# The final RMSNorm of a hybrid decoder: sums spread by one product, the root by Ln and Exp, VectorE's factors in PSUM, and the steps of a finished chunk written earlier

## The chip, the cores and the metric

The kernel runs on one core of a Trainium2 chip. The metric is the device time of one execution, in microseconds; smaller is better. The core's engines work side by side, each on its own list of instructions in order: TensorE (PE in the profile) multiplies matrices from SBUF into PSUM, VectorE (DVE), ScalarE (ACT) and GpSimd (POOL) work element by element, and SyncE (SP) issues the transfers between the chip's memory and SBUF. They wait for each other through semaphores.

## What is computed

One inference step of a small decoder: a Mamba-2 layer with a squared-ReLU MLP, then a layer of sliding-window attention with another MLP, for 1024 new prompt positions and 64 sample positions, each 1024 features wide. All that matters here is the very end, the norm of the stream after the second MLP:

```python
def rmsnorm(x, w):
    xf = x.astype(jnp.float32)
    xf = xf * lax.rsqrt(jnp.mean(xf * xf, axis=-1, keepdims=True) + EPS)
    return (xf * w.astype(jnp.float32)).astype(x.dtype)
...
    y_prompt = rmsnorm(hp, final_norm_w)
    y_sample = rmsnorm(hs, final_norm_w)
```

So each position needs the mean of the squares of its 1024 features, the inverse root of it, and a scaling of the 1024 features by that factor and by the weights.

## The kernel before

**Layout.** Features lie on the 128 partitions, positions along the free dimension: the stream `hh` is 128 x 8 x 1088, eight feature tiles (numbered u = 0 to 7) of 1088 positions. The positions are cut into three chunks, c = 0, 1 and 2, of 384, 384 and 320. A sum over features is therefore a sum over the eight tiles (VectorE) and over the partitions (a product with a matrix of ones on TensorE).

**The stage around the change.** The last block of the second MLP's down projection (`down_block`, `down`, `down_unit`, line 949) makes, for each chunk and tile, a group of twelve products into one PSUM tile `g`; the operands are split in two parts, so each of four weights enters through three products (lines 205 to 207). VectorE then adds the PSUM tile to `hh` (line 949); that is called eviction below. Tiles 0 to 3 are made for all chunks in turn; then the tail makes tiles 4 to 7 of chunk 0, of chunk 1, of chunk 2. The PSUM tiles `g` come from a ring of seven banks (`gps`, with three banks and four more), handed out in the order in which the code is written; a bank is free again when its last reader is through.

**What hangs on each eviction.** `final(c, u)` is called after each. After every odd tile up to 5 ScalarE squares a pair of tiles (`n3`), VectorE adds the squares into `acc`, and ScalarE multiplies the pair by its weights; tiles 6 and 7 are squared one by one into `sq` and get their weights later. For chunk 2, the square of tile 7 is not added but enters the sum over partitions as a second operand.

**The end of a chunk.** `final_rs` sums over the partitions: three products per chunk, each with 128 positions of `acc` as the stationary operand and a column of ones (line 1770), so that the sums lie as columns, 128 positions on the partitions. ScalarE takes the square root of the 128 x 3 values (line 1772), VectorE the reciprocal (1773), and three scalings of the identity give diagonal matrices `dg` (1776). `final_bc` multiplies ones with these (1787), which spreads each position's factor over all 128 rows of a PSUM tile, and ScalarE copies that into `rs` in SBUF (1789). `final_scale` multiplies a pair of tiles by the factor and sends it out (SyncE, line 1803): the pairs k = 4 and k = 0 are GpSimd's, k = 6 (with its weights, line 1799) and k = 2 are VectorE's (1802); for chunk 2, k = 0 is VectorE's as well. GpSimd always reads the factor from `rs`; VectorE reads it from `rs` for chunks 0 and 1, from PSUM for chunk 2.

**What sets the order.** The code is written in one sequence, and a scheduler with its own cost model places each engine's instructions, with the order of writing as the priority. Before, the end of chunk c - 1 is written at three places of chunk c: `final_rs` at tile 5, `final_bc` and all scalings at tile 7. The end of chunk 2 follows at its own tile 7.

Of the kernel before, what the change touches and what calls it, by code (L numbers as in the profile page):

```python
# [11 lines left out]
AF = mybir.ActivationFunctionType  # L12
ALU = mybir.AluOpType
# [4 lines left out]
P = 128  # L18
D = 1024
# [123 lines left out]
class Kernel:  # L143
# [1578 lines left out]
    def final(self, c, u, hts, chs):  # L1722

        nc = self.nc
        n = chs[c][1]
        h = hts[c]
        if c > 0 and u == 5:
            self.final_rs(c - 1, chs)
        if c > 0 and u == 7:
            self.final_bc(c - 1, chs)  # L1730
        if u % 2 and u < 6:
            sq = self.n3()[:, :, :n]
            nc.scalar.activation(out=sq, in_=h[:, u - 1:u + 1, :n], func=AF.Square)
            if u == 1:
                acc = self.fin("acc", 3, n)
                self.acc[c] = [acc]
                nc.vector.tensor_tensor(out=acc, in0=sq[:, 0], in1=sq[:, 1], op=ALU.add)
            else:
                acc = self.acc[c][0]
                for j in range(2):  # L1740
                    nc.vector.tensor_tensor(out=acc, in0=acc, in1=sq[:, j], op=ALU.add)

            for k in (u - 1, u):
                nc.scalar.mul(out=h[:, k, :n], in_=h[:, k, :n], mul=self.ncol(4)[:, k:k + 1])
        elif u >= 6:
            sq = self.fin("sq", 2, n)
            nc.scalar.activation(out=sq, in_=h[:, u, :n], func=AF.Square)
            if u == 6 or c < 2:
                nc.vector.tensor_tensor(out=self.acc[c][0], in0=self.acc[c][0], in1=sq, op=ALU.add)
            else:  # L1750
                self.acc[c].append(sq)
        if c > 0 and u == 7:
            for k, e in ((4, nc.gpsimd), (6, nc.vector), (0, nc.gpsimd), (2, nc.vector)):
                self.final_scale(c - 1, k, e, hts, chs)
        if c == 2 and u == 7:
            self.final_rs(c, chs)
            self.final_bc(c, chs)
            for k, e in ((6, nc.vector), (4, nc.gpsimd), (0, nc.vector), (2, nc.vector)):
                self.final_scale(c, k, e, hts, chs)

    def final_rs(self, c, chs):

        nc = self.nc
        n = chs[c][1]
        ms = self.gps()[:, :3]
        r = self.fin("rt", 2, 3)
        for b in range(3):
            o = min(b * P, n - P)
            for q, a in enumerate(self.acc[c]):
                nc.tensor.matmul(out=ms[:, b:b + 1], lhsT=a[:, o:o + P], rhs=self.ones_d[:, 0:1], start=(q == 0),  # L1770
                                 stop=(q == len(self.acc[c]) - 1))
        nc.scalar.activation(out=r, in_=ms, func=AF.Sqrt, bias=self.eps1)
        nc.vector.reciprocal(out=r, in_=r)
        dg = self.fin("dg", 2, 3 * P).rearrange("p (b t) -> p b t", b=3)
        for b in range(3):
            nc.vector.tensor_scalar(out=dg[:, b], in0=self.ident, scalar1=r[:, b:b + 1], scalar2=float(D),
                                    op0=ALU.mult, op1=ALU.mult)
        self.acc[c] = dg

    def final_bc(self, c, chs):  # L1780

        nc = self.nc
        n = chs[c][1]
        ps = self.gps()[:, :n]
        for b in range(3):
            o = min(b * P, n - P)
            nc.tensor.matmul(out=ps[:, o:o + P], lhsT=self.ones_d, rhs=self.acc[c][:, b], start=True, stop=True)
        rs = self.fin("rs", 2, n)
        nc.scalar.copy(out=rs, in_=ps)
        self.acc[c] = {nc.gpsimd: rs, nc.vector: ps if c == 2 else rs}  # L1790

    def final_scale(self, c, k, e, hts, chs):
        nc = self.nc
# [290 lines left out]
```

## Time and profile before

| | |
|---|---|
| median of the runs | 2852.68 us (3 runs, 2851.2 to 2852.72) |
| the profiled execution's own time | 2850.09 us |
| its span, first to last instruction | 2848.4 us |
| mean granted TensorE clock | 0.995 |
| output transfers of the final norm | 8 of 384 KB, 4 of 320 KB |
| last eviction starts | 2832.20 us |
| last scaling ends (VectorE) | 2843.79 us |

Times inside the span are counted from its start. A timeline row gives start, length, engine, line of the kernel, operation, tile written and tiles read, and in brackets the idle time of the engine before it and whom it waited for. A group of rows gives the count, the busy time with the mean in ns, and the idle time before. Products are pipelined: a row of TensorE is longer than the distance to the next, and a float32 product appears as two rows. KB in the table are of 1024 bytes.

### The profile page before, as it was taken

The numbers are of one execution on the slowest core, as the hardware profiler recorded it, in microseconds if no ns is written. First come the engines' busy times: TensorE is split into PE (matmuls) and PEld (weight loads), VectorE is DVE, ScalarE is ACT, GpSimd is POOL, SyncE is SP. The second block draws the span as 40 slices with busy tenths as digits, with TensorE's granted clock in tenths as the row PEclk, the third lists the DMA queues.
The fourth block names the chain that finished last, engine by engine and source line by source line (L and its number), as shares of the span: only waits on it lengthen the run. The fifth ranks groups of instructions, "written<-read, shape, count | busy, mean of one in ns | idle before, by whom it ended". The sixth has DMA issues, their size and how long they took to land.

```text
span 2848.4 us, 51380 instructions
## 1 busy us (share of the span) xinstructions
PE 2791.9 (98%) x19895; PEld 2692.3 (95%) x19895; DVE 2078.6 (73%) x3615; ACT 1389.7 (49%) x2719; POOL 471.0 (17%) x659
## 2 busy tenths in 40 slices
PE   8999999989999999999999999999999999999997
PEld 7999999979989999999999999988989999999997
DVE  6788888886768786666578875676688666567786
ACT  6555555545654255445343334555555444523333
POOL 3355555551000100000000022110110000000011
PEclk9999999999999999999999999999999999999999
DMA  4344444457655224533654523446553354533432
GB/s 140 94 127 123 119 124 124 124 145 249 246 206 181 91 93 133 176 133 131 246 197 174 192 99 104 165 171 240 182 194 110 132 183 146 226 111 127 145 113 71
DMA packets 219468, 433.42 MB, mean 152 GB/s; under 512 B 30728, under 2 KB 128392, under 8 KB 216648
## 3 DMA queue, kind: packets, MB, share of 16 engines
q1 hardware_dynamic: 219224, 430.14, 45.5%
q8 instruction: 157, 2.57, 0.4%
q14 instruction: 87, 0.71, 0.1%
HBM read 302.71 MB, written 128.32 MB: 151 GB/s over the span
## 4 chain that ended last, share of the span: by engine, by line
PE 86%; DVE 5%; DMA 5%; ACT 2%; issue 2%; POOL 0%; SPq 0%; DVEq 0%; ACTq 0%; POOLq 0%
PE g L206 12%; PE g L205 12%; PE g L207 12%; PE ma L205 4%; PE ma L207 4%; PE ma L206 4%; PE mc L207 4%; PE mc L206 4%; PE mc L205 4%; PE md L206 3%; PE md L207 3%; PE mb L207 3%; PE mb L206 3%; PE mb L205 3%; PE md L205 3%
## 5 line engine op out<-in xcount | busy, mean ns | idle before, releaser
L205 PE MATMUL g<-S,w 128*128 128x384 f32 (+2 forms) x1584 | 529.7, 335 | 4.7 <-DMA w<-ws_up 3.2
L206 PE MATMUL g<-S,w 128*128 128x384 f32 (+2 forms) x1584 | 531.5, 336 | 0.0
L207 PE MATMUL g<-S,w 128*128 128x384 f32 (+2 forms) x1584 | 527.4, 333 | 0.0
L205 PEld LDWEIGHTS g<-S,w 128*128 128x128 f32 x1584 | 298.5, 188 | 7.3 <-issue 4.7
L1078 ACT CAST w<-s 128x384 fp32r<-128x384 f32 (+1 forms) x272 | 150.6, 557 | 315.3 <-PE mc L207 57.9
L206 PEld LDWEIGHTS g<-S,w 128*128 128x128 f32 x1584 | 298.8, 189 | 3.0 <-issue 2.4
L207 PEld LDWEIGHTS g<-S,w 128*128 128x128 f32 x1584 | 299.4, 189 | 2.1 <-issue 1.7
L1329 POOL TENSOR_TENSOR hh<-hh,us 128x552 f32<-128x552 f32 (+1 forms) x24 | 42.5, 1790 | 1531.0 <-DVE us L1305 877.0
L205 PE MATMUL ma<-S,w 128*128 128x276 f32 (+1 forms) x808 | 234.1, 290 | 5.0 <-DVE us L1305 3.8
L206 PE MATMUL ma<-S,w 128*128 128x276 f32 (+1 forms) x808 | 233.8, 289 | 0.3 <-DVE S L1267 0.3
L207 PE MATMUL ma<-S,w 128*128 128x276 f32 (+1 forms) x808 | 234.0, 290 | 0.0
L1079 DVE TENSOR_TENSOR w<-s,w 128x384 fp32r<-128x384 f32 (+1 forms) x272 | 166.4, 615 | 80.8 <-ACT w L1078 80.7
L1078 ACT CAST w<-raw 128x384 fp32r<-128x384 f32 (+1 forms) x204 | 112.2, 557 | 183.9 <-PE mc L207 57.8
L171 ACT CAST w<-raw 128x1024 fp32r<-128x1024 f32 x96 | 100.7, 1049 | 142.3 <-PE g L206 52.8
L206 PE MATMUL g<-R,w 128*128 128x384 f32 (+2 forms) x480 | 158.3, 330 | 0.0
L205 PEld LDWEIGHTS ma<-S,w 128*128 128x128 f32 x808 | 152.5, 189 | 5.8 <-issue 4.1
L205 PE MATMUL g<-R,w 128*128 128x384 f32 (+2 forms) x480 | 157.8, 329 | 0.0
L207 PE MATMUL g<-R,w 128*128 128x384 f32 (+2 forms) x480 | 157.7, 329 | 0.0
L172 DVE TENSOR_TENSOR w<-raw,w 128x1024 fp32r<-128x1024 f32 x96 | 122.4, 1275 | 47.1 <-ACT w L171 32.3
L206 PEld LDWEIGHTS ma<-S,w 128*128 128x128 f32 x808 | 152.8, 189 | 0.5 <-DVE S L1267 0.5
L207 PEld LDWEIGHTS ma<-S,w 128*128 128x128 f32 x808 | 152.6, 189 | 0.0
L206 PE MATMUL mc<-S,w 128*128 128x276 f32 (+1 forms) x512 | 148.0, 289 | 0.0
(493 smaller groups left out, 8515.9 us busy)
## 6 DMA issues: line engine op xcount, KB each, us to landing
raw<-in_w_up_dram SPq DMA_DIRECT2D x64, 512.0 KB
raw<-in_w_in_dram SPq DMA_DIRECT2D x48, 512.0 KB
raw<-in_w_downs_dram SPq DMA_DIRECT2D x64, 384.0 KB
w<-ws_o SPq DMA_DIRECT2D x46, 512.0 KB
w<-ws_q SPq DMA_DIRECT2D x40, 512.0 KB
ab<-acs_d SPq DMA_DIRECT2D x64, 256.0 KB
S<-t_d SPq DMA_DIRECT2D x18, 828.0 KB
S<-t_e SPq DMA_DIRECT2D x18, 816.0 KB
```

The costliest lines, as they stand in the source:

```text
L171: nc.scalar.copy(out=wh, in_=raw)
L172: nc.vector.tensor_tensor(out=wl, in0=raw, in1=wh.bitcast(F32), op=ALU.subtract)
L205: mm(out=out, lhsT=wh, rhs=xh, start=(first and k == 0), stop=False)
L206: mm(out=out, lhsT=wh, rhs=xl, start=False, stop=False)
L207: mm(out=out, lhsT=wl, rhs=xh, start=False, stop=(k == n - 1))
L1078: self.last_hi = nc.scalar.copy(out=t[:, 0], in_=src).ins
L1079: self.last_lo = nc.vector.tensor_tensor(out=t[:, 1], in0=src, in1=t[:, 0].bitcast(F32), op=ALU.subtract).ins
L1329: e.tensor_tensor(out=to, in0=to, in1=uv, op=ALU.add)
```

## The change

`final_rs` now makes the sums with ones as the stationary operand and the whole chunk of `acc` as the moving one: one product gives each position's mean on all 128 rows of a PSUM tile (line 1766 of the new code; for chunk 2 two products, `acc` and `sq`). ScalarE takes Ln of it into `rs` (1767), then Exp of -0.5 times that, once into the PSUM tile (1768) and once into `rs` (1769). `final_bc`, the square root, the reciprocal, the diagonals and their products are gone. VectorE reads the factor from PSUM in every chunk, GpSimd from `rs`. `final_rs` of chunk c - 1 is now written at tile 4 of chunk c, the scalings of pairs 4 and 6 at tile 5, those of pairs 0 and 2 at tile 6.

```diff
@@ final
-        if c > 0 and u == 5:
-            self.final_rs(c - 1, chs)
-        if c > 0 and u == 7:
-            self.final_bc(c - 1, chs)
...
-        if c > 0 and u == 7:
-            for k, e in ((4, nc.gpsimd), (6, nc.vector), (0, nc.gpsimd), (2, nc.vector)):
+        if c > 0 and u == 4:
+            self.final_rs(c - 1, chs)
+        if c > 0 and u in (5, 6):
+            for k, e in ((4, nc.gpsimd), (6, nc.vector)) if u == 5 else ((0, nc.gpsimd), (2, nc.vector)):
                 self.final_scale(c - 1, k, e, hts, chs)
         if c == 2 and u == 7:
             self.final_rs(c, chs)
-            self.final_bc(c, chs)
@@ final_rs
-        ms = self.gps()[:, :3]
-        r = self.fin("rt", 2, 3)
-        for b in range(3):
-            o = min(b * P, n - P)
-            for q, a in enumerate(self.acc[c]):
-                nc.tensor.matmul(out=ms[:, b:b + 1], lhsT=a[:, o:o + P], rhs=self.ones_d[:, 0:1], start=(q == 0),
-                                 stop=(q == len(self.acc[c]) - 1))
-        nc.scalar.activation(out=r, in_=ms, func=AF.Sqrt, bias=self.eps1)
-        nc.vector.reciprocal(out=r, in_=r)
-        dg = self.fin("dg", 2, 3 * P).rearrange("p (b t) -> p b t", b=3)
...
-    def final_bc(self, c, chs):
...
         ps = self.gps()[:, :n]
-        for b in range(3):
-            o = min(b * P, n - P)
-            nc.tensor.matmul(out=ps[:, o:o + P], lhsT=self.ones_d, rhs=self.acc[c][:, b], start=True, stop=True)
         rs = self.fin("rs", 2, n)
-        nc.scalar.copy(out=rs, in_=ps)
-        self.acc[c] = {nc.gpsimd: rs, nc.vector: ps if c == 2 else rs}
+        last = len(self.acc[c]) - 1
+        for q, a in enumerate(self.acc[c]):
+            nc.tensor.matmul(out=ps, lhsT=self.ones_d, rhs=a, start=(q == 0), stop=(q == last))
+        nc.scalar.activation(out=rs, in_=ps, func=AF.Ln, bias=self.eps1)
+        nc.scalar.activation(out=ps, in_=rs, func=AF.Exp, scale=-0.5)
+        nc.scalar.activation(out=rs, in_=rs, func=AF.Exp, scale=-0.5)
+        self.acc[c] = {nc.gpsimd: rs, nc.vector: ps}
```

On VectorE, the stretch in which chunk 0 is scaled stands as follows before (`g` with a number is one PSUM tile of products, in order of its writing: 31032 is chunk 1's tile 7, 31081 and 31067 are chunk 2's tiles 5 and 4; `rs_31050` is chunk 0's factor):

```order
L949 TENSOR_TENSOR hh_27466<-hh_27466,g_31032 128x384
L1749 TENSOR_TENSOR acc_30758<-acc_30758,sq_31052 128x384
L949 TENSOR_TENSOR hh_27466<-hh_27466,g_31081 128x320
L1799 SCALAR_TENSOR_TENSOR hh_27466<-hh_27466,nv_72,rs_31050 128x384 x2
L1802 TENSOR_TENSOR hh_27466<-hh_27466,rs_31050 128x384 x2
L949 TENSOR_TENSOR hh_27466<-hh_27466,g_31067 128x320
```

And so now (31016, 30990 and 31039 are chunk 1's tiles 6, 5 and 7, 31056 and 31076 chunk 2's tiles 4 and 5; `g_30984` is chunk 0's factor):

```order
L949 TENSOR_TENSOR hh_27466<-hh_27466,g_31016 128x384
L1779 SCALAR_TENSOR_TENSOR hh_27466<-hh_27466,nv_72,g_30984 128x384 x2
L1782 TENSOR_TENSOR hh_27466<-hh_27466,g_30984 128x384 x2
L949 TENSOR_TENSOR hh_27466<-hh_27466,g_30990 128x384
L949 TENSOR_TENSOR hh_27466<-hh_27466,g_31039 128x384
L949 TENSOR_TENSOR hh_27466<-hh_27466,g_31056 128x320
L1737 TENSOR_TENSOR acc_30758<-acc_30758,n3_31004 128x384 x2
L949 TENSOR_TENSOR hh_27466<-hh_27466,g_31076 128x320
```

Chunk 0's scalings have moved from behind chunk 1's last eviction and one of chunk 2 to ahead of two evictions of chunk 1.

On ScalarE, the end of the program, before (31149 is the square of chunk 2's tile 7, 31147 and 31181 are the factors of chunks 1 and 2):

```order
L1747 ACTIVATE sq_31149<-hh_27466 128x320
L1789 COPY rs_31147<-g_31143 128x384
L1772 ACTIVATE rt_31164<-g_31163,eps_67 128x3
L1789 COPY rs_31181<-g_31177 128x320
L2080 UNCONDITIONAL_BRANCH
```

And now (31139 is that square; `g_31070` and `rs_31071` belong to chunk 1, `g_31141` and `rs_31142` to chunk 2):

```order
L1767 ACTIVATE rs_31071<-g_31070,eps_67 128x384
L1743 ACTIVATE sq_31139<-hh_27466 128x320
L1768 ACTIVATE g_31070<-rs_31071 128x384
L1769 ACTIVATE rs_31071<-rs_31071 128x384
L1767 ACTIVATE rs_31142<-g_31141,eps_67 128x320
L1768 ACTIVATE g_31141<-rs_31142 128x320
L1769 ACTIVATE rs_31142<-rs_31142 128x320
```

Two operations of 128x384 and 128x320 have become six, and the last square stands between chunk 1's Ln and its Exp.

On TensorE, the end of the program now, behind the last products of the down projection (where before stood chunk 1's three products of line 1787, chunk 2's six of line 1770 and its three of line 1787):

```order
L205 MATMUL g<-R_24162,w 128x320
L206 MATMUL g<-R_24162,w 128x320
L207 MATMUL g<-R_24162,w 128x320
L1766 MATMUL g<-acc,ones_r 128x384
L1766 MATMUL g<-acc,ones_r 128x320
L1766 MATMUL g<-sq,ones_r 128x320
```

Chunk 1's sum, which before stood among chunk 2's products, has moved behind them. SyncE's order changes at one place: chunk 1's pair 0 is issued after two pairs of chunk 2, where before it stood ahead of all four.

More of the change, by code (lines that the diff above doesn't have):

```diff
@@ L1764, in final_rs @@
         n = chs[c][1]
-        ms = self.gps()[:, :3]
-        r = self.fin("rt", 2, 3)
-        for b in range(3):
-            o = min(b * P, n - P)
-            for q, a in enumerate(self.acc[c]):
-                nc.tensor.matmul(out=ms[:, b:b + 1], lhsT=a[:, o:o + P], rhs=self.ones_d[:, 0:1], start=(q == 0),
-                                 stop=(q == len(self.acc[c]) - 1))
-        nc.scalar.activation(out=r, in_=ms, func=AF.Sqrt, bias=self.eps1)
-        nc.vector.reciprocal(out=r, in_=r)
-        dg = self.fin("dg", 2, 3 * P).rearrange("p (b t) -> p b t", b=3)
-        for b in range(3):
-            nc.vector.tensor_scalar(out=dg[:, b], in0=self.ident, scalar1=r[:, b:b + 1], scalar2=float(D),
-                                    op0=ALU.mult, op1=ALU.mult)
-        self.acc[c] = dg
-    def final_bc(self, c, chs):
-        nc = self.nc
-        n = chs[c][1]
         ps = self.gps()[:, :n]
-        for b in range(3):
-            o = min(b * P, n - P)
-            nc.tensor.matmul(out=ps[:, o:o + P], lhsT=self.ones_d, rhs=self.acc[c][:, b], start=True, stop=True)
         rs = self.fin("rs", 2, n)
-        nc.scalar.copy(out=rs, in_=ps)
-        self.acc[c] = {nc.gpsimd: rs, nc.vector: ps if c == 2 else rs}
+        last = len(self.acc[c]) - 1
[5 more added lines that the diff above has]
+        self.acc[c] = {nc.gpsimd: rs, nc.vector: ps}
     def final_scale(self, c, k, e, hts, chs):
```

## The prediction

> **What bounds the kernel now.** I read the page first, then the chain of waits and the busy times microsecond by microsecond over the last 30 us, where the diff acts, then single rows there. The page says whose kernel this is:
>
> ```profile
> span 2848.4 us, 51380 instructions
> PE 2791.9 (98%) x19895; PEld 2692.3 (95%) x19895; DVE 2078.6 (73%) x3615; ACT 1389.7 (49%) x2719; POOL 471.0 (17%) x659
> ```
>
> TensorE is busy for 98% of the span, so only what stands in its stream, or behind its last product, can move the time. The chain from 2832 us on shows what stands behind (start, us, engine, line):
>
> ```profile
> 2833.59 1.88 DVE hh L1799 x2
> 2835.47 2.53 DVE hh L1802 x2
> 2838.12 0.82 DVE dg L1776
> 2838.99 1.66 PE g L1787 x6
> 2840.73 0.43 ACT rs L1789
> 2841.19 0.55 DVE hh L1799
> ```
>
> While VectorE scales chunk 1 (1.88 + 2.53 us), chunk 2's sums are long there; the diagonal tiles that spread them (L1776) queue behind these scalings, and chunk 2's factors exist only at 2841.2. Then comes the way out of the chip. Per stretch (us; sum, then PE, PEld, DVE, ACT, POOL busy; TensorE's granted clock; DMA share; GB/s), with the issues of the output transfers:
>
> ```profile
> 2834.00:2835.00 1.00, 0.64 (x6) 0.56 (x5) 1.00 (x2) 0.26 (x1) 1.00 (x1) 0.81 0.06 16
> 2836.00:2837.00 1.00, 0.00 (x0) 0.00 (x0) 1.00 (x2) 0.00 (x0) 1.00 (x2) 0.50 0.63 223
> 2837.00:2838.00 1.00, 0.00 (x0) 0.00 (x0) 1.00 (x2) 0.00 (x0) 1.00 (x2) 0.50 1.00 358
> 2840.00:2841.00 1.00, 0.64 (x3) 0.34 (x2) 0.00 (x0) 0.27 (x1) 0.00 (x0) 0.50 1.03 372
> 2843.00:2844.00 1.00, 0.00 (x0) 0.00 (x0) 0.79 (x2) 0.00 (x0) 0.00 (x0) 0.50 0.89 307
> 2844.00:2845.00 1.00, 0.00 (x0) 0.00 (x0) 0.00 (x0) 0.00 (x0) 0.00 (x0) 0.50 1.04 356
> 2845.00:2846.00 1.00, 0.00 (x0) 0.00 (x0) 0.00 (x0) 0.00 (x0) 0.00 (x0) 0.50 1.03 352
> 2846.00:2847.00 1.00, 0.00 (x0) 0.00 (x0) 0.00 (x0) 0.00 (x0) 0.00 (x0) 0.50 0.85 296
> 2835.50 1.22 SPq L1803 DMA_DIRECT2D out_dram<-hh  x2
> 2842.22 2.27 SPq L1803 DMA_DIRECT2D out_dram<-hh  x4
> ```
>
> Chunk 2's four transfers are issued from 2842.22 on and run at full DMA share. 307 at a rate of 354 (the mean of the two full stretches) means a start at 2843.13, 0.9 us after the issue; chunk 1's 223 of 365 gives 2836.4, the same 0.9. The 1.31 MB end at about 2846.85; the span ends 1.55 us later. So the end is not VectorE's last scaling but a queue of transfers: an end moves when the first transfer of an unbroken queue starts sooner.
>
> **The change part by part.** The products first (TensorE rows, start and us; the two L342 rows are float32 products of 128x384 by the same ones):
>
> ```profile
> 2817.57 0.72 PE L1770 MATMUL g<-ones_r,acc 128*128 128x1 f32 x6
> 2818.16 0.42 PE L206 MATMUL g<-R,w 128*128 128x384 f32 x1
> 2822.94 0.38 PE L1787 MATMUL g<-dg,ones_r 128*128 128x128 f32 x2
> 2823.90 0.31 PE L207 MATMUL g<-R,w 128*128 128x320 f32 x1
> 2825.95 0.72 PE L1770 MATMUL g<-ones_r,acc 128*128 128x1 f32 x6
> 2826.53 0.39 PE L205 MATMUL g<-R,w 128*128 128x320 f32 x1
> 2829.40 0.31 PE L207 MATMUL g<-R,w 128*128 128x320 f32 x1
> 25.40 0.81 PE L342 MATMUL xms<-xsq,ones_r 128*128 128x384 f32 x2
> 25.75 0.61 PE L577 MATMUL g<-S,w 128*128 128x336 f32 x1
> 26.20 0.81 PE L342 MATMUL xms<-xsq,ones_r 128*128 128x384 f32 x2
> ```
>
> Removed from the stream ahead of the last product: the column sums of chunk 0 (0.59 us to the next product) and of chunk 1 (0.58), and chunk 0's three spreading products: 0.96 between 2822.94 and 2823.90, less two products of 320 columns (0.147 each, below), 0.67. Together 1.84. Added: one product of 384 columns. From one L342 to the next lie 0.80 us with one product of 336 columns (0.155) between, so 0.645, and 0.81 to its own end. Net -1.2 us. The last product starts at 2829.40 and frees TensorE 0.147 later, 2829.55 (1.76 us for a tile of twelve); in the new order 2828.35. Chunk 1's sum now follows there, where chunk 1's spreading stood before.
>
> ScalarE and VectorE come next (groups: busy us, mean ns, then idle before; for L271 and L1713 min/median/max ns; the one with a start in front is from the timeline):
>
> ```profile
> L271 ACT ACTIVATE rs<-ms,eps x5: 541/581/582, 1000.7 to 1741.9; 128x384 f32<-128x384 f32 x4, 128x336 f32<-128x336 f32 x1
> L272 ACT ACTIVATE rs<-rs 128x384 f32<-128x384 f32 x4 | 2.1, 522 | 0.0
> L1747 ACT ACTIVATE sq<-hh 128x320 f32<-128x320 f32 x2 | 0.9, 469 | 0.3 <-DVE hh L949 0.3
> L1799 DVE SCALAR_TENSOR_TENSOR hh<-hh,nv,rs 128x384 f32<-128x384 f32 x4 | 4.6, 1198 | 0.8 <-ACT rs L1789 0.8
> L1799 DVE SCALAR_TENSOR_TENSOR hh<-hh,nv,g 128x320 f32<-128x320 f32 x2 | 1.0, 546 | 1.9 <-ACT rs L1789 1.9
> L1802 DVE TENSOR_TENSOR hh<-hh,rs 128x384 f32<-128x384 f32 x4 | 5.3, 1354 | 0.0
> L1802 DVE TENSOR_TENSOR hh<-hh,g 128x320 f32<-128x320 f32 x4 | 1.7, 481 | 0.0
> L1802 POOL TENSOR_TENSOR hh<-hh,rs 128x384 f32<-128x384 f32 x8 | 10.0, 1281 | 51.8 <-ACT rs L1789 51.8
> 2841.23 1.68 POOL L1802 TENSOR_TENSOR hh<-hh,rs 128x320 f32<-128x320 f32 x2 [2.38 <-ACT rs L1789]
> L1713 POOL TENSOR_TENSOR S<-hs,S x24: 860/1012/1473, 1888.9 to 2095.1; 128x384 fp32r<-128x384 f32 x16, 128x320 fp32r<-128x320 f32 x8
> ```
>
> With the factor from SBUF (rs), beside GpSimd's scalings, VectorE takes 1198 and 1354 ns; with it from PSUM (g) 546 and 481 for 320 columns, and the weighted pair of these (2841.19 to 2842.2) lies wholly beside GpSimd's 1.68 us. I take 1.15 us for two weighted scalings of 384 (1.01 for the pair of 320, by columns and rounded down), 1.1 for the two plain ones; the far end is the contended 2.75 and 2.66.
>
> The Trainium skill speaks against this edit: "VectorE: DVE Perf Modes", section "Rules for kernel authors", advises to copy PSUM to SBUF first where many operations follow; its cost table there adds 62 cycles at 0.96 GHz per PSUM read, by which two scalings would be an estimated 0.13 us later and the gain 5.8. The rows side with the edit.
>
> Chunk 1's path, step by step, from TensorE free at 2828.35: its sum ends 2829.16 (0.81); hand-over 0.09 (in the chain, 2840.65 to 2840.73), Ln 0.58: 2829.83; the last Square stands ahead of Exp on ScalarE (0.47): 2830.30; Exp 0.52 into PSUM: 2830.82. No row has ScalarE writing PSUM: bounds 0.43 (the chain's copy out of PSUM) and 0.58 (Ln). VectorE's first pair ends at 2832.0. Its first output transfer is then issued, against 2835.50 before: 3.5 us sooner. Bytes move from 2832.9.
>
> Is the queue unbroken? It holds chunk 1's four (1.573 MB at 365: 4.3 us) and chunk 2's four (1.311 at 354: 3.7), 8.0 us, to 2840.9. VectorE ends its other chunk 1 pair at 2833.1, ready to move at 2834.0, when the first is through (2834.0). GpSimd starts after the second Exp at 2831.4; at 1.01 us each its pairs end 2833.4 and 2835.4 (at 1.28, as now, 2836.5), its last pair (1.68) by 2837.1 to 2838.2; needed at the latest at 2839.1 (2840.9 less 0.9 and its own 0.9). Chunk 2's sums need the last Square (2830.3), end near 2831.1, and Ln and Exp give factors at 2832.4, while VectorE is at chunk 1 until 2833.1; it ends all at 2835.8. Everything behind the first pair is hidden by the transfers; that includes GpSimd, Ln, Exp and the diagonal steps saved for chunk 2. Uncovered, GpSimd would be late by at most 0.9.
>
> Chunk 0, moved sooner, adds one wait: VectorE stands before the weighted scaling until Exp (product 2817.57, Ln 2818.5, Exp done 2819.6), then scales until 2821.9. Queued behind are evictions of three tiles, one ready at 2820.5, late by 1.4 us; TensorE waits for none, since the code gives seven banks in turn, and chunk 2's third tile, which takes the factor's bank, is reached at 2824.8 (2828.35 less 24 products). Slack 3.0 us. Its four transfers are gone before 2832. The sqrt table's load vanishes from an idle ScalarE: nothing.
>
> Sum: 2832.9 + 8.0 + 1.55 = 2842.45 against 2848.4, -5.95 us. The profiled execution took 2850.09, so 2844.1; the median of the runs shown is 2852.68, 2.6 above it, and carries over: 2846.7. Bounds of the unknown terms: Exp -0.1 to +0.1, pair of scalings -0.1 to +0.3, product 0 to +0.3, rate of the queue -0.2 to +0.3, overlaps ±0.3, and ±0.8 since the three runs before span 1.5: ±1.4 together, 2845.3 to 2848.1. A measurement here tells 0.2% (5.7 us) from no change; the forecast lies almost on that line.
>
> **The rivals.** (A) The queue runs faster. The early loads moved more than the outputs do:
>
> ```profile
> 8.00:10.00 2.00, 2.00 (x4) 0.68 (x2) 1.00 1.00 393
> ```
>
> At 390, 2.88 MB take 7.4 us: 2846.1. Against: those are loads; every full stretch of outputs shows 352 to 372.
>
> (B) VectorE is as slow from PSUM as it was from SBUF, because GpSimd runs beside it. Then the first pair ends 2833.6, the second 2836.25, and as SyncE issues in order, GpSimd's pair waits behind; chunk 2's pairs come at 2838.5, 2840.75, 2843.0, and the last transfer ends 2845.75: span 2847.3, -1.1, 2851.6. Against: the weighted g pair above, taken with GpSimd busy.
>
> (C) Ln and Exp each load a table. Earlier in the kernel a Ln does:
>
> ```profile
> L816 ACT ACT_TABLE_LOAD  x7: 1283/1283/1283, 669.3 to 825.5; - x7
> ```
>
> Two loads ahead of chunk 1's Exp put the first transfer 2.6 us later, and two more open a gap of 0.6 before chunk 2's: -2.8, 2849.9. Against: L272 follows L271 with no idle time, and the new order lists no load. The Trainium skill, "ScalarE: Activation LUTs", section "Table sets: the hidden batching unit", names one set with both functions; by that this rival falls.
>
> (D) Slower: VectorE's new wait at chunk 0 starves TensorE of its bank. It decides once chunk 0's scalings end over 3.0 us late, after 2824.8. Then TensorE idles, and some 5 us after the last dense product its clock sinks (0.81, then 0.50 in the rows above), so the 24 products left (3.5 us) double. Losing 5.95 + 5.7 takes a stall of 8.2: 2858.4 or more. Even contended scalings are only 3.3 late.
>
> **How the numbers follow.** Forecast 0.69, A 0.12, B 0.08, C 0.08, D 0.03. Of the forecast's ±1.4 about six tenths lie beyond -5.7: 0.41, with A 0.53 faster; the rest, 0.28, with B and C, 0.44 the same; D 0.03 slower. The range 2845.1 to 2850.0 takes in the forecast's spread, A but for its tail, and C; it leaves out B, D and thin ends.
>
> **What would show it.** In the new profile: TensorE's last product of twelve at 2828.2; one float32 product per chunk of 0.65 us in the stream; no table load at the end; VectorE's chunk 1 scalings at 0.5 to 0.65 us from g; the first chunk 1 transfer issued at 2832.0; DMA share near 1.0 from 2833 to 2841 without a hole. A hole there, a PE idle time before chunk 2's third tile, or scalings over 1 us would make the prediction wrong.

## The result, and the profile after

| | before | after |
|---|---|---|
| median of 15 executions each | 2852.09 us | 2844.63 us |
| lowest and highest of these | 2846.97, 2855.86 us | 2840.47, 2851.48 us |
| ratio of the times | | 0.9975 (95%: 0.9968 to 0.9981) |
| span of the profiled execution | 2848.4 us | 2838.8 us |

The change makes the kernel faster by 0.25%, 7.1 us with an interval of 5.4 to 9.1. The forecast of -5.95 us lies inside that interval; the forecast time of 2846.7 us is 2.1 above the median, and the range (from 2845.1) just misses it.

The page of after; TensorE's share is what it was:

```profile
span 2838.8 us, 51305 instructions
PE 2788.0 (98%) x19861; PEld 2686.4 (95%) x19861; DVE 2069.2 (73%) x3603; ACT 1391.5 (49%) x2721; POOL 468.8 (17%) x659
```

The spans of the two profiles differ by 9.6 us, and the first thing to ask is where. The change touches nothing before the last tile of chunk 0 is evicted. That eviction, in the timeline of before and then of after:

```profile
2812.40 0.56 DVE L949 TENSOR_TENSOR hh<-hh,g 128x384 f32<-128x384 f32 x1 [0.31 <-PE g L207]
```

```profile
2809.04 0.56 DVE L949 TENSOR_TENSOR hh<-hh,g 128x384 f32<-128x384 f32 x1 [0.31 <-PE g L207]
```

Call its start the anchor, what lies ahead of it the head, and what lies behind it, up to the span's end, the tail. The head differs by 3.4 us, the tail is 36.0 us before and 29.8 after: -6.2. The experiments below go by the tail.

The tail in after, from TensorE's last product of the block on: the rows of TensorE and then those of ScalarE in the timeline (of the four rows of line 1766 the first two are chunk 1's sum, the others the first of chunk 2's):

```profile
2824.69 0.31 PE L207 MATMUL g<-R,w 128*128 128x320 f32 x1
2824.84 1.34 PE L1766 MATMUL g<-acc,ones_r 128*128 128x384 f32 x4
2825.68 0.58 ACT L1767 ACTIVATE rs<-g,eps 128x384 f32<-128x384 f32 x1 [1.08 <-PE g L1766]
2826.16 0.46 ACT L1743 ACTIVATE sq<-hh 128x320 f32<-128x320 f32 x1
2826.52 0.48 ACT L1768 ACTIVATE g<-rs 128x384 f32<-128x384 f32 x1
2827.04 0.52 ACT L1769 ACTIVATE rs<-rs 128x384 f32<-128x384 f32 x1
```

Sum, Ln, the last Square, Exp: the very steps, in the order, that the prediction listed. Neither a diagonal nor a table load is left. VectorE's scalings of chunk 1 in the timeline, with the first output transfer behind them:

```profile
2827.04 1.14 DVE L1779 SCALAR_TENSOR_TENSOR hh<-hh,nv,g 128x384 f32<-128x384 f32 x2 [1.51 <-ACT g L1768]
2828.09 1.01 DVE L1782 TENSOR_TENSOR hh<-hh,g 128x384 f32<-128x384 f32 x2
2828.21 0.37 SPq L1783 DMA_DIRECT2D out_dram<-hh  x1
```

The stretches around the queue (sum, then PE, PEld, DVE, ACT, POOL busy, granted clock, DMA share, GB/s):

```profile
2829.00:2830.00 1.00, 0.00 (x0) 0.00 (x0) 1.00 (x4) 0.08 (x1) 1.00 (x2) 1.00 0.91 319
2830.00:2831.00 1.00, 0.00 (x0) 0.00 (x0) 1.00 (x4) 0.00 (x0) 1.00 (x2) 0.87 1.03 367
...
2836.00:2837.00 1.00, 0.00 (x0) 0.00 (x0) 0.00 (x0) 0.00 (x0) 0.00 (x0) 0.50 1.04 361
2837.00:2838.00 1.00, 0.00 (x0) 0.00 (x0) 0.00 (x0) 0.00 (x0) 0.00 (x0) 0.50 0.14 47
```

A pair takes 1.14 and 1.01 us (GpSimd is at its own scalings from 2827.70 on, so the first pair runs partly beside it and the second wholly), the first transfer of chunk 1 is issued at 2828.21, bytes move from about 2829.13 (319 of 365) to 2837.13 without a hole (every stretch between is at a share of 1.02 to 1.04), 8.0 us, and the span ends 1.67 us later.

### The profile page after: what moved, and what is told of

It is laid out like the page before. It is cut to its first block, busy times and chain, and to the rows that moved or that the text cites. A ratio compares the mean times of both kernels' runs of the same rounds, so it can differ in the third digit from the quotient of the medians.

```text
span 2838.8 us, 51305 instructions
## 1 busy us (share of the span) xinstructions
PE 2788.0 (98%) x19861; PEld 2686.4 (95%) x19861; DVE 2069.2 (73%) x3603; ACT 1391.5 (49%) x2721; POOL 468.8 (17%) x659
## 4 chain that ended last, share of the span: by engine, by line
PE 86%; DMA 5%; DVE 5%; ACT 2%; issue 2%; POOL 0%; SPq 0%; POOLq 0%; ACTq 0%; DVEq 0%
PE g L206 12%; PE g L205 12%; PE g L207 12%; PE ma L205 4%; PE ma L207 4%; PE ma L206 4%; PE mc L207 4%; PE mc L206 4%; PE mc L205 4%; PE md L206 3%; PE md L207 3%; PE md L205 3%; PE mb L207 3%; PE mb L206 3%; PE mb L205 3%
```

## The experiments

The theory: the whole gain is made in the tail, where chunk 1's first transfer starts an unbroken queue sooner; the difference of the heads is chance. The rival: the edit also makes the earlier code faster, so that the profile's 9.6 us are real. A second question is which of the change's parts earns the 6.2 us. It has three: the arithmetic (one product, Ln and Exp for column sums, square root, reciprocal and diagonals), VectorE's factors in PSUM, and the sooner writing places.

All profiles in one table, each with its own anchor, in us. The ratio is that to runs of before on the same chip, with its 95% interval; the last three runs of the table were executed only once. Each line is one profile, and the runs come from several chips; how far a tail repeats is known from before and after alone.

| run | clock | anchor | span | tail | ratio |
|---|---|---|---|---|---|
| before | 0.995 | 2812.40 | 2848.4 | 36.0 | |
| before again | 0.994 | 2811.46 | 2847.6 | 36.1 | 0.9998 (0.9987 to 1.0008) |
| after | 0.997 | 2809.04 | 2838.8 | 29.8 | 0.9975 (0.9968 to 0.9981) |
| after again | 0.992 | 2823.55 | 2853.3 | 29.8 | 0.9979 (0.9968 to 0.9990) |
| old places | 0.994 | 2815.85 | 2845.3 | 29.5 | 0.9974 (0.9964 to 0.9984) |
| old places, more on GpSimd | 0.994 | 2813.29 | 2843.1 | 29.8 | 0.9980 (0.9971 to 0.9989) |
| factors in SBUF | 0.993 | 2817.82 | 2850.4 | 32.6 | 0.9983 (0.9973 to 0.9992) |
| factors in PSUM alone | 0.993 | 2816.72 | 2848.6 | 31.9 | 0.9981 (0.9971 to 0.9992) |
| places alone | 0.992 | 2814.44 | 2857.3 | 42.9 | 1.0023 (1.0013 to 1.0033) |
| places and factors | 0.993 | 2814.22 | 2850.8 | 36.6 | 1.0003 (0.9992 to 1.0015) |
| sum 12 ahead | 0.994 | 2817.23 | 2845.7 | 28.5 | 0.9978 (0.9969 to 0.9988) |
| Ln and Exp alone | 0.992 | 2821.93 | 2857.8 | 35.9 | |
| arithmetic alone | 0.992 | 2818.32 | 2853.8 | 35.5 | |
| one transfer less | 0.994 | 2818.54 | 2847.1 | 28.6 | |

### Both kernels once more

Nothing is edited here.

> The kernel before, unchanged, timed against itself. The head is the time from the span's start to the start of the eviction (L949) of the last tile of chunk 0, code that the change does not touch: 2812.40 us in the profile of before and 2809.04 in that of after; the tail is from there to the span's end, 36.0 and 29.8 us. Theory (the whole gain lies in the tail, the 3.4 us of the head are chance): ratio 1.000 with an interval of about 0.0006 to each side, tail 36.0 us within 0.5, and a head that lies anywhere between about 2808 and 2815 us. Rival (the edit also makes the earlier code faster): head within 0.5 us of 2812.4, since the same code then takes the same time.

> The changed kernel, unchanged, once more. Theory (gain in the tail alone, -6.2 us by the two profiles, -5.95 as forecast): ratio 0.9978 (0.9973 to 0.9983), that is -6.2 us with 1.4 to each side; tail 29.8 us within 0.5; head anywhere between about 2808 and 2815 us. Rival (the edit also earns 3.4 us in the head): ratio 0.9966 (-9.6 us) and a head within 0.5 us of 2809.0.

The anchor of after, this time:

```profile
2823.55 0.56 DVE L949 TENSOR_TENSOR hh<-hh,g 128x384 f32<-128x384 f32 x1 [0.31 <-PE g L207]
```

The same kernel is 14.5 us later at the same instruction, well outside the 2808 to 2815 us that I had expected of chance, and its tail is the same to 0.02 us: 2853.3 less 2823.55 is 29.75, 2838.8 less 2809.04 is 29.76. Before repeats its tail to 0.15. So the rival is refuted: a head of 2809 is no property of the changed kernel, and of the profile's 9.6 us 3.4 are chance. It also shows what the tail is good for: it repeated to 0.02 and 0.15 us, where the ratios of medians have intervals about 4 to 7 us wide. All timed ratios agree with the tails within these.

Where do the 14.5 us come from? Cut into stretches of 100 us, the two profiles show different granted clocks in eight of 28, lower in the repetition by 0.01 to 0.03 each; 0.15 in all would be 15 us, as an estimate for a stream bound by TensorE. Two of them (sum, PE busy, granted clock, DMA share, GB/s), in after and then in its repetition:

```profile
1900.00:2000.00 100.00, 96.92 (x742) 1.00 0.64 226
...
2600.00:2700.00 100.00, 99.19 (x789) 1.00 0.34 112
```

```profile
1900.00:2000.00 100.00, 97.76 (x724) 0.97 0.68 239
...
2600.00:2700.00 100.00, 96.06 (x751) 0.98 0.34 112
```

In all eight TensorE is not busy throughout: there the granted clock is 0.95 to 0.99 in the slower execution and 0.97 to 1.00 in the quicker one. The Trainium skill, "TensorE: Matmul & The Clock Gate", Part 1, calls the activity window of 3.4 us that sets the clock free-running, so that the point at which the clock changes varies from run to run. The rows go with that; no run here isolates it, and the cause of the heads' spread stays argued.

### The new arithmetic at the old places

```diff
@@ final (after)
+        if c > 0 and u == 5:
+            self.final_rs(c - 1, chs)
...
-        if c > 0 and u == 4:
-            self.final_rs(c - 1, chs)
-        if c > 0 and u in (5, 6):
-            for k, e in ((4, nc.gpsimd), (6, nc.vector)) if u == 5 else ((0, nc.gpsimd), (2, nc.vector)):
+        if c > 0 and u == 7:
+            for k, e in ((4, nc.gpsimd), (6, nc.vector), (0, nc.gpsimd), (2, nc.vector)):
```

> The new arithmetic at the old writing places: sums when tile 5 of the next chunk is done, scalings at its tile 7. The scheduler then puts the sum of chunk 1 into TensorE's stream 24 products before its end (24 by 0.145 us, 3.5 us sooner than in after), and chunk 1's scalings on VectorE ahead of the last eviction. Theory (the tail is set by how soon chunk 1's first transfer starts, and then by an unbroken queue): chunk 1's sum waits for its last accumulation, which comes about 0.4 us late; first chunk-1 scaling about 2.1 us sooner than in after, the last eviction 2 to 3 us later behind 2.2 us of scalings; chunk 2's first transfer is ready about 1 us after the queue has run dry, so the tail is 28.6 us (27.6 to 29.6), against 29.8 of after and 36.0 of before. Rival 1 (the sooner writing places earn part of the gain): tail 30.5 to 33 us. Rival 2 (chunk 2's chain sets the end, since its last eviction is 2 to 3 us later): tail 31.5 us.

29.5 us: the sooner places earn nothing, which refutes rival 1. The time lies in the theory's range, near its end, and the hole of about 1 us that the theory foresaw in the queue is there; rival 2, in which chunk 2's chain costs more, is not reached with its 31.5. TensorE waits for chunk 1's last accumulation, and chunk 2's last eviction starts behind chunk 1's scalings:

```profile
2829.24 0.91 PE L1766 MATMUL g<-acc,ones_r 128*128 128x384 f32 x2 [0.95 <-DVE acc L1747]
...
2835.06 0.47 DVE L949 TENSOR_TENSOR hh<-hh,g 128x320 f32<-128x320 f32 x1
```

The stretches (columns as above) show the price:

```profile
2838.00:2839.00 1.00, 0.00 (x0) 0.00 (x0) 0.97 (x3) 0.47 (x1) 0.42 (x1) 0.50 0.97 352
2839.00:2840.00 1.00, 0.00 (x0) 0.00 (x0) 1.00 (x4) 0.00 (x0) 1.00 (x2) 0.50 0.03 9
2840.00:2841.00 1.00, 0.00 (x0) 0.00 (x0) 0.63 (x2) 0.00 (x0) 0.26 (x1) 0.50 1.04 356
```

Chunk 1's first scaling starts 16.5 us behind the anchor instead of 18.0 (1.5 us sooner, where I had 2.1); but from 2839 to 2840 the queue is empty, since chunk 2's last eviction starts at 19.2 instead of 16.0. What is won at the front of the queue is lost in its middle.

### The old places, and more scalings on GpSimd

```diff
@@ final (the run before)
-            for k, e in ((4, nc.gpsimd), (6, nc.vector), (0, nc.gpsimd), (2, nc.vector)):
+            for k, e in ((4, nc.gpsimd), (6, nc.vector), (0, nc.gpsimd), (2, nc.gpsimd)):
```

> As the run before, and in chunks 0 and 1 GpSimd scales three of the four pairs instead of two, so that VectorE has 1.0 us less ahead of the last eviction. Theory: GpSimd's six tiles of chunk 1 at 1.0 us end when the queue has about written the first three pairs; chunk 2's first transfer is ready when the queue runs dry; tail 28.0 us (27.2 to 29.0), the best of the four: 8 us below before, ratio 0.9972. Rival (GpSimd's six tiles set the end): six tiles from the factors on, 6.0 us, and then chunk 2's two at 0.87 us: tail 29.5 us or more.

29.8: the rival was right in its time and in the engine that is waited for. GpSimd scales chunk 1's six tiles and chunk 2's two in one row, and the queue runs dry once more, for over half of the stretch from 2835 to 2836, while it waits for GpSimd's pairs of chunk 1 (the timeline, then the stretch):

```profile
2830.53 7.66 POOL L1782 TENSOR_TENSOR hh<-hh,rs 128x384 f32<-128x384 f32 x8 [1.80 <-ACT rs L1769]
```

```profile
2835.00:2836.00 1.00, 0.00 (x0) 0.00 (x0) 1.00 (x4) 0.00 (x0) 1.00 (x2) 0.50 0.44 152
```

Its last tile does not set the end: it is done at 2838.19, 4.9 us ahead of it. What sets the end is the queue, which is unbroken only from about 2835.6 on.

### The factors back in SBUF

```diff
@@ final_rs (after)
-        nc.scalar.activation(out=ps, in_=rs, func=AF.Exp, scale=-0.5)
+        if c == 2:
+            nc.scalar.activation(out=ps, in_=rs, func=AF.Exp, scale=-0.5)
         nc.scalar.activation(out=rs, in_=rs, func=AF.Exp, scale=-0.5)
-        self.acc[c] = {nc.gpsimd: rs, nc.vector: ps}
+        self.acc[c] = {nc.gpsimd: rs, nc.vector: ps if c == 2 else rs}
```

> After, but VectorE reads the factors of chunks 0 and 1 from rs in SBUF, which GpSimd reads too, so the Exp into PSUM is left out there; chunk 2 stays as it is. The anchor is the start of the eviction of the last tile of chunk 0; the tail runs from it to the span's end (36.0 and 36.1 us in the two profiles of before, 29.8 and 29.8 in those of after). Theory (the factors from PSUM are what keeps VectorE's scalings at 0.5 to 0.6 us each beside GpSimd): the scalings of chunks 0 and 1 go back to 0.9 to 1.4 us each as in before, 3.2 us more for chunk 0's pairs; 1.5 us of that is taken up by VectorE's idle time before chunk 1's scalings, the rest delays chunk 1's sum; tail 32.9 us (31.5 to 35). Rival (it is the single product and the Ln and Exp that earn the gain, the place of the factors little): tail 29.8 to 30.6 us.

32.6 for an expected 32.9. Here are the groups of scalings of after, and below them those of this run (busy us, mean ns, idle before):

```profile
L1782 POOL TENSOR_TENSOR hh<-hh,rs 128x384 f32<-128x384 f32 x8 | 7.8, 1011 | 50.1 <-ACT rs L1769 50.1
L1779 DVE SCALAR_TENSOR_TENSOR hh<-hh,nv,g 128x384 f32<-128x384 f32 x4 | 2.3, 612 | 4.0 <-ACT g L1768 4.0
L1782 DVE TENSOR_TENSOR hh<-hh,g 128x384 f32<-128x384 f32 x4 | 2.0, 547 | 0.0
```

```profile
L1783 POOL TENSOR_TENSOR hh<-hh,rs 128x384 f32<-128x384 f32 x8 | 10.0, 1284 | 50.4 <-ACT rs L1770 50.4
L1783 DVE TENSOR_TENSOR hh<-hh,rs 128x384 f32<-128x384 f32 x4 | 5.3, 1355 | 0.0
L1780 DVE SCALAR_TENSOR_TENSOR hh<-hh,nv,rs 128x384 f32<-128x384 f32 x4 | 4.7, 1204 | 3.4 <-ACT rs L1770 3.4
```

Nothing but the place of the factor (and the Exp that writes it) differs, and VectorE takes 2 to 2.5 times as long, GpSimd a quarter more. In these scalings the two engines hold each other up when VectorE reads both operands from SBUF, and not when one lies in PSUM. That is what the Trainium skill says of two SBUF inputs in "SBUF — State Buffer", section "Who interferes with whom", and the trace agrees.

### The factors in PSUM alone

```diff
@@ final_bc (before)
-        self.acc[c] = {nc.gpsimd: rs, nc.vector: ps if c == 2 else rs}
+        self.acc[c] = {nc.gpsimd: rs, nc.vector: ps}
```

> Before, with one thing taken from the change: VectorE reads the spread factors of chunks 0 and 1 from PSUM too, as it did in chunk 2. Theory: scalings of 1.1 us a pair instead of 1.9 to 2.75; chunk 1's first transfer 0.8 us sooner, the reciprocal of chunk 2 2.2 us sooner and with it the end: tail 33.8 us (33.0 to 35.0), -2.2 of the 6.2 us. Rival (the factors alone earn nearly all of it): tail 31 us or less. Rival (they earn nothing, because the chain over the diagonal sets the end): tail 35.5 to 36.2 us.

31.9, below the theory's range and above the rival's 31: this one line earns 4.2 us. I had counted only chunk 1's shorter scalings. Chunk 0's, 3.3 us shorter, bring forward chunk 1's reciprocal, diagonals and scalings too. What is left is the way over the diagonals, slowed by GpSimd beside it (the chain of waits):

```profile
2831.54 1.51 DVE dg L1776 x3
...
2835.55 1.14 DVE hh L1799 x2
2836.69 0.93 DVE hh L1802 x2
...
2837.74 1.87 DVE dg L1776 x2
...
2839.66 1.24 PE g L1787 x4
```

Chunk 1's scalings start 18.8 us behind the anchor (before: 21.2), and chunk 2's diagonals follow them at once, but each step stands in turn. Three diagonals take 0.68 us in chunk 0, where GpSimd is idle, and 2.06 in chunk 2, where it is at chunk 1's scalings, though such a step reads one tile and a column of factors only, both in SBUF:

```profile
2825.29 0.68 DVE L1776 TENSOR_SCALAR dg<-ident,rt 128x128 f32<-128x128 f32 x3
...
2837.74 2.06 DVE L1776 TENSOR_SCALAR dg<-ident,rt 128x128 f32<-128x128 f32 x3
```

### The places alone, and with the factors

```diff
@@ final (before)
-        if c > 0 and u == 5:
-            self.final_rs(c - 1, chs)
-        if c > 0 and u == 7:
-            self.final_bc(c - 1, chs)
...
+        if c > 0 and u == 4:
+            self.final_rs(c - 1, chs)
+            self.final_bc(c - 1, chs)
+        if c > 0 and u in (5, 6):
+            for k, e in ((4, nc.gpsimd), (6, nc.vector)) if u == 5 else ((0, nc.gpsimd), (2, nc.vector)):
```

The second run has this and the one line of the run before.

> Before, with one thing taken from the change: the sums, their spreading and the scalings of chunks 0 and 1 are written at the new, sooner places; square root, reciprocal, diagonal and the factors in SBUF stay. The scheduler then puts chunk 1's scalings on VectorE ahead of chunk 2's accumulations. Theory (the places by themselves earn nothing): chunk 1's spreading ends as late as before, behind the last product of the stream, and chunk 2's accumulations wait on VectorE for 4.5 us of scalings, though before had idle time and other steps there: tail 36.0 us (35.0 to 37.5). Rival (the sooner places earn part of the gain): tail 32 to 34.5 us.

> Before, with two things taken from the change: the new writing places and VectorE's factors from PSUM; square root, reciprocal, diagonal and spreading products stay. With the places alone the tail was 42.9 us, since chunk 2's accumulations stood behind 4.5 us of chunk 1's scalings and TensorE waited; the factors shorten chunk 0's scalings by 3.3 us and chunk 1's by 2.35 (as measured with the factors alone). Theory (each part is worth what it takes off VectorE's queue ahead of chunk 2's sum, so the two add up): 42.9 less 3.3 less 2.35, tail 37.2 us (36.0 to 38.8), still above before. Rival (the places are good as soon as the factors lie in PSUM): tail 31.9 us or less, the time of the factors alone.

42.9 and 36.6. The places alone cost 6.8 us where I expected nothing; I had foreseen the order on VectorE, but not its price. TensorE's rows of the first:

```profile
2832.91 0.77 PE L1786 MATMUL g<-dg,ones_r 128*128 128x128 f32 x2 [2.90 <-ACT sq L1743]
...
2844.30 0.59 PE L1769 MATMUL g<-ones_r,acc 128*128 128x1 f32 x2 [7.27 <-DVE acc L1745]
```

Chunk 1's spreading products now stand ahead of products of the block and wait there, and chunk 2's sum waits 7.27 us for accumulations that VectorE has behind 4.5 us of scalings. With the factors in PSUM the places still cost 4.7 (36.6 against 31.9), as the sum of the parts had it (37.2).

### The arithmetic: the root alone, and the whole of it

```diff
@@ final_rs (before)
-        nc.scalar.activation(out=r, in_=ms, func=AF.Sqrt, bias=self.eps1)
-        nc.vector.reciprocal(out=r, in_=r)
+        nc.scalar.activation(out=r, in_=ms, func=AF.Ln, bias=self.eps1)
+        nc.scalar.activation(out=r, in_=r, func=AF.Exp, scale=-0.5)
```

The second run is the new arithmetic at the old places, with the edit of "The factors back in SBUF" besides.

> Before, with one thing taken from the change: the root of the 128x3 sums by Ln and Exp instead of Sqrt and a reciprocal on VectorE; the diagonal, the spreading products, SBUF factors and the places stay. Times from the anchor (start of the eviction of chunk 0's last tile); tail of before 36.0 and 36.1 us. Theory (the root by itself earns almost nothing): the table load of 1.28 us at chunk 0 goes, which delays nothing that the end waits for; on the way to chunk 2's factors an Exp of 0.26 us stands for a reciprocal of 0.16; tail 36.0 us (35.3 to 36.4). Rival (it takes a table load before each Exp, 1.28 us): tail 37.4 us or more.

> Before, with two things taken from the change: the single product over the accumulated squares and the root by Ln and Exp over all rows; the factors of chunks 0 and 1 stay in SBUF and the writing places stay the old ones. With factors from PSUM beside it, at the same old places, the tail is 29.45 us; with both parts at the new places it is 29.8, and there the SBUF factors took it to 32.6. Theory (the parts overlap, each alone earns over half of the 6.3 us): tail 32.4 us (31.5 to 34.0). Rival (this part alone is worth no more than what the factors alone left over, 31.9 less 29.8 is 2.1 us): tail 33.8 us or more.

The root alone: 35.9, nothing, as expected. The whole arithmetic alone: 35.5 where I expected 32.4; the rival (33.8 or more) was right. It earns 0.5 us by itself. I had assumed that the parts overlap and each alone earns over half; instead the arithmetic needs the factors in PSUM. The waits of TensorE from 2818 us on (total us, times, longest):

```profile
PE g L1766 <- DVE acc L1747: 6.4, 2, 3.6
```

The single product reads `acc` in TensorE's stream, and `acc` is complete only when VectorE is through with the scalings of the chunk before: with factors in SBUF chunk 1's is late by 2.8 us, chunk 2's by 3.6, and the stream waits. With factors in PSUM chunk 1's wait is 0.95 and the same arithmetic earns 2.4 us more than the factors alone (31.9 to 29.5).

### The queue as the bound

```diff
@@ final_scale (after)
-        nc.sync.dma_start(out=self.o["y"][:, k:k + 2, o:o + n], in_=hv)
+        if (c, k) != (1, 0):
+            nc.sync.dma_start(out=self.o["y"][:, k:k + 2, o:o + n], in_=hv)
```

> After, without the transfer of chunk 1's pair 0 (tiles 0 and 1 of that chunk are not written; 393 KB of the 2.88 MB that leave in the last queue). Theory (from chunk 1's first transfer on the end is set by an unbroken queue at about 365 GB/s): 1.08 us less, tail 28.7 us (28.5 to 28.9). Rival (the last scalings of chunk 2 set the end, and the queue has slack): tail 29.6 to 29.9 us, unchanged.

28.6, that is 1.2 us less for 393 KB. The queue is the bound: VectorE and GpSimd end at their old distances from the anchor (22.6 and 24.2 us), and the span still shortens by about the transfer's own time, 1.08 at 365 GB/s.

### A better place for chunk 1's sum

```diff
@@ final (after)
-        if c > 0 and u == 4:
+        if c > 0 and u == 6:
             self.final_rs(c - 1, chs)
-        if c > 0 and u in (5, 6):
-            for k, e in ((4, nc.gpsimd), (6, nc.vector)) if u == 5 else ((0, nc.gpsimd), (2, nc.vector)):
+        if c > 0 and u == 7:
+            for k, e in ((4, nc.gpsimd), (6, nc.vector), (0, nc.gpsimd), (2, nc.vector)):
```

> The new arithmetic with other writing places: the sums of a chunk when tile 6 of the next is done, the scalings at its tile 7. The scheduler puts chunk 1's sum 12 products before the end of TensorE's stream, where its last accumulation is there in time (in the run with the old places it waited 0.95 us). Theory (the first chunk-1 transfer sets the start of an unbroken queue of 8.0 us): chunk 1's sum 1.6 us sooner than in after, Ln, Square and Exp behind it as in after, first scaling at 16.6 us from the anchor against 18.0, a hole of about 0.3 us in the queue while GpSimd's first pair is awaited; tail 28.7 us (28.2 to 29.4), the shortest of all. Rival (chunk 2's chain sets the end, since its last eviction stands behind chunk 1's scalings): tail 29.4 us or more, as with the old places (29.45).

28.5, the shortest tail, 1.3 below after. Chunk 1's sum waits for nothing, its first scaling starts 16.3 us behind the anchor, and the queue has one hole of note, some 0.34 us of the stretch in which chunk 2's transfers begin (the timeline, then the stretch):

```profile
2833.50 1.13 DVE L1779 SCALAR_TENSOR_TENSOR hh<-hh,nv,g 128x384 f32<-128x384 f32 x2
```

```profile
2840.00:2841.00 1.00, 0.00 (x0) 0.00 (x0) 1.00 (x3) 0.00 (x0) 0.68 (x1) 0.50 0.66 225
```

By the times it cannot be told from after (0.9978 and 0.9975 to 0.9979): 1.3 us is 0.05%, and each of these intervals is 0.06% or more wide to either side. That it is better rests on the tail alone.

## Why the prediction was right in its mechanism and missed the time

**The sum.** In the prediction's own terms, counted from the anchor (2812.40 and 2809.04 taken off; the measured times are those of the timeline's rows):

| step | predicted | measured |
|---|---|---|
| TensorE free for chunk 1's sum | 15.95 | 15.80 |
| Ln starts | 16.85 | 16.64 |
| Exp into PSUM starts | 17.90 | 17.48 |
| it has ended | 18.42 | 17.96 |
| first chunk 1 transfer issued | 19.6 | 19.17 |
| its bytes move | 20.5 | 20.1 |
| queue empty | 28.5 | 28.1 |
| end of the span | 30.05 | 29.76 |

The product added (0.81 to its own end), the scalings from PSUM, 0.9 us from issue to bytes, the 8.0 us of the queue: each as forecast. The sum is 0.3 us too cautious. Up to the end of Exp it is 0.46, in three places. The first is the products removed. The prediction took each chunk's column sums to cost the time up to the next product, 0.59 and 0.58 us; but that product's successor is late too. Two products of before, one ahead of chunk 0's column sums and the second one behind them:

```profile
2817.40 0.33 PE L205 MATMUL g<-R,w 128*128 128x384 f32 x1
...
2818.42 0.34 PE L207 MATMUL g<-R,w 128*128 128x384 f32 x1
```

They start 1.02 us apart; less two products of 0.17, 0.68 is left for the sums, and for chunk 1's 0.67 by the same count. So the net is -1.35 us and not -1.2: the last product of the block starts 15.65 us behind the anchor, 17.00 before. The second is the hand-over from the sum to Ln, 0.03 instead of 0.09. The third, 0.25, is ScalarE: the Square starts 0.10 before the row of Ln has ended, Exp 0.10 before that of the Square, and Exp lasts 0.48 instead of 0.52. The way from the last byte to the end, 1.67 instead of 1.55, gives 0.12 back. The bounds for Exp and for overlaps held; for the products that leave there was none.

**The step that failed** is the last bound: "±0.8 since the three runs before span 1.5", and with it the forecast time, which carried that median over. Three executions of before had spanned 1.5 us; 15 of them span 8.9, those of after 11.0, and a kernel's head moves by 14.5 us with no edit at all. 0.3 of the missing 2.1 us is the sum; 0.6 is the median of before, 2852.68 then and 2852.09 now; the other 1.2 lies between the difference of the medians (7.5) and that of the tails (6.2 to 6.4), well inside an interval of 5.4 to 9.1; no run here tells it from chance. The base alone would have been enough: counted from 2852.09, the same range begins at 2844.5 and takes the result in. In the repetition the ratio is 0.9979, 6.0 us. The standard deviation of one execution is 2.3 us in the 15 of before; an estimate from it for a median of three is 1.7 us (1.25 times 2.3 over the root of three). Eight times in ten such a median lies within 1.28 times that, 2.1 us; with 2.1 in place of 0.8 the ±1.4 become ±2.4 (by squares), and the range would have begun at 2844.3. The figures ahead of the prediction gave a hint that was passed over: the profiled execution took 2850.09 us and stood 1.1 us outside the three.

**The rivals.** A, a quicker queue: its stretches show 353 to 367 GB/s, no 390. B, contention from PSUM as well: refuted, 612 and 547 ns, the plain ones with GpSimd busy throughout. C, a table load for Ln and for Exp: none in after's tail, nor in the run with the root alone, where Ln, Exp and Square follow each other without one. The Trainium skill, "ScalarE: Activation LUTs", section "Table sets: the hidden batching unit", names one set with both, and these traces agree. D, a starved TensorE: TensorE waits for nothing in after until chunk 2's last Square (0.49 us). Its mechanism is real in the neighbours, with another releaser: with the arithmetic alone TensorE waits 6.4 us for accumulations that are late behind VectorE's scalings, with the places alone 7.3 for the same, and 2.9 ahead of chunk 1's spreading products.

**The page weighed in the prediction.** The Trainium skill, "VectorE: DVE Perf Modes", section "Rules for kernel authors", advises to copy PSUM to SBUF first where many operations follow. The measurement says otherwise: here factors in SBUF cost 2.8 us of the tail (32.6 against 29.8), since the price of reading SBUF beside GpSimd, 1204 and 1355 ns instead of 612 and 547, is far above that of reading PSUM. Of the estimated 0.13 us for reading PSUM nothing shows: with GpSimd idle, an addition of this size takes 0.56 us with one operand in PSUM (line 949) and 0.56 with both in SBUF (line 1745).

**The parts.** The prediction costed them as one path and did not ask what each is worth. By the tail, in us:

| tail | factors in SBUF | factors in PSUM |
|---|---|---|
| old arithmetic, old places | 36.0 | 31.9 |
| old arithmetic, new places | 42.9 | 36.6 |
| new arithmetic, old places | 35.5 | 29.5 |
| new arithmetic, new places | 32.6 | 29.8 |

Factors in PSUM earn 2.8 to 6.3 us in every row. The new places earn 2.9 in one case only, and cost or do nothing in the others. The arithmetic is worth 0.5 or 2.4 at the old places and pays most at the new ones, which are harmful without it.

## What to carry to other kernels

When an edit acts in one stretch, pick an instruction just ahead of it that the edit can't reach and compare from there: here that repeated to 0.15 us, where medians of a dozen executions leave 2 to 3 us open to either side; and take the spread of the time from many executions, not from three. At the end of a kernel, write down when the first byte of the last unbroken queue leaves, then look for holes in the queue: a sooner front is worth only what the chain of the last chunk can follow. Parts of an edit that meet in one engine's queue do not add up, so test them in pairs before keeping or dropping one.

## What the runs showed of the hardware

The same kernel reached the same instruction at 2809.0 us and at 2823.6 us, with mean granted clocks of 0.997 and 0.992, while the 30 us behind it repeated to 0.02 us. A VectorE scaling of 128x384 with both operands in SBUF took 1204 to 1355 ns beside GpSimd, which itself went from 1011 to 1284 ns; with one operand in PSUM it took 547 to 612 ns. Three scalings of a 128x128 tile by a column of factors, both in SBUF, took 0.68 us with GpSimd idle, and 2.06 beside it. On ScalarE a step that does not depend on the one ahead started before that one's row had ended: the Square 0.48 us after the start of a Ln of 0.58, the Exp 0.36 us after that of a Square of 0.46.
